# Feature-major rotation, score levels on more column groups and side-by-side gate products in a two-layer decoder trunk

## The chip, the core and the metric

The kernel runs on one core of one Trainium2 chip. The core has five instruction queues: TensorE (PE, matrix products into the PSUM banks), VectorE (DVE), ScalarE (ACT), GpSimd (POOL) and SyncE (SP, which here only starts DMAs). The metric is the device time of one execution in microseconds (us). All data are 32-bit floats, and the big products run as three products of split operands, as told below.

## The reference

A decoder trunk of two layers for one sequence of 1024 tokens and a model width of 1024. In each layer the normalised and modulated input is projected once, and four branches of four heads each read parts of that projection:

```
proj = jnp.einsum('bld,de->ble', h, w_in[layer])
y_a = hgrn2_branch(aq, af, ai, ag, ...)      # vector decay, exact within chunks
y_b = retention_branch(rq, rk, rv, rg, ...)  # scalar decay, rotary q and k
y_c = ssd_branch(...)                        # Mamba-2
y_d = gla_branch(gq, gk, gv, gg, glr, w_gk2, ...)
x = x + gate * jnp.einsum('ble,ed->bld', concat(y_a..y_d), w_out[layer])
```

Three of its formulas matter here. The rotation of the retention's q and k pairs feature d with feature d + 64 of a head of 128:

```
cat([t1 * cos - t2 * sin, t1 * sin + t2 * cos])
```

The gates of GLA come from a product of rank 16, `gk = lr_in @ w_gk2 + b_gk2` (16 columns into 256), and then `log_sigmoid(gk) / 16`. And the branches with a vector decay (HGRN2 and GLA) need scores in which each pair of positions s < t of a chunk has its own decay per channel; the kernel forms these by levels of blocks of size h = 1, 2, 4, ... 64: at each level the second half of every block of 2h looks at the first half.

## The kernel before

**Two kinds of projection.** A weight unit of 128 output columns can be projected feature-major (`proj_f`, L423): the result has features on the partitions and 512 tokens in each of two PSUM banks, by 48 matmuls of 512 columns (8 slices of the model width, 2 halves of the tokens, 3 products). Or 256 columns are projected token-major (`proj_t`, L454): tokens on the partitions, four PSUM banks, by 192 matmuls of 256 columns. The three products are hi times hi, hi times lo and lo times hi of the split weights (`split`, L402: ACT casts, DVE subtracts) and the split input (hh, hl). The PSUM pool `pp` has four banks for projections, for the output projection and a few transposes. Four more hold the mixers' products: tags `sc` (two), `po` and `ms` (one each). SBUF tiles of 128 x 1024 come from the pool `big` of eleven, tiles of 128 x 512 from `mid` of five.

**The order on TensorE is written by hand.** Projections and output projections are generators in a queue (`ready`); a mixer is a generator that yields a number of nanoseconds, and `fill` issues so much of the queue before the mixer goes on. So a mixer's small products stand between those of a projection, and a `yield 2500` means "issue about 2.5 us of queued products here". The other engines' queues are ordered by the scheduler of the framework.

**The retention branch, before.** `ret_qk` (L867) projects q and k of a head together, token-major, one `proj_t` of 256 columns. For each of four PSUM banks ACT copies q and k out (L877), DVE makes four products with cos and sin (L881 to L884, 128 x 128 each, twice), and POOL forms the difference and the sum (L885, L886). `ret_mix` (L891) then transposes q and k, 16 transposes of 128 x 128 on TensorE (L897) into `sc`, `ms`, `sc`, `po`, copies them out, scales k by its decay on DVE (L900), yields 1200, makes the scores (L910), multiplies them by the decay mask on DVE (L912) and goes into `scan` (L651), which makes the outputs and the running state. Each head's q and k are projected while the mixer of the head before runs: the queue holds `ret_qk` of the next head, then the projection of its v and gate (`vg_proj`). Head 0 is projected while the second group of the SSD branch runs in `ssd_mix` (L1028). There POOL weights the inputs of each chunk (L1069) and DVE carries the state (L1113 to L1127).

**Scores by levels, before.** `vector_scores` (L546) is called with one head of HGRN2 (nh = 1, moving operand 32 or 64 columns at the levels in question) and with two heads of GLA side by side (nh = 2, 64 or 128 columns). At h up to 16, keys of 32 positions are the weights, and the products of four blocks of a chunk go to PSUM partitions 0, 32, 64 and 96 (L584). At h = 32 (L592) they go to partitions 0 and 64 alone. At h = 64 (L601) all go to partitions 0 to 63, for GLA in two banks one after the other. ACT copies the results into the score matrix (L636, L641).

**Gates of GLA, before.** `gla_gates` (L756): 8 transposes (L762) bring the 16 columns onto partitions 0 to 15, ACT copies each half out, and after a `yield 900` four products of 16 rows by 512 columns follow (L777), each in its own bank of `sc`, with `yield 700` and two DVE instructions (L778, L779) behind each. Then ACT takes Exp and Ln, DVE subtracts (L786), ACT takes Exp again, and a `yield 8000` follows. The output projection, whose results DVE adds to the residual stream (L1164), is what fills these pauses.

**The end of a layer.** The last head of the retention, then the output projection of the last two branches' columns in `out_tiles` (L1171, products L1159), whose weights POOL multiplies by the gate (L1148).

Of the kernel before, what the change touches and what calls it, by code (L numbers as in the profile page):

```python
# [21 lines left out]
P = 128  # L22
# [6 lines left out]
C = 128  # L29
# [41 lines left out]
for _h in range(4):  # L71
    _t(("rqk", _h), RQ + 128 * _h, RK + 128 * _h)
    _t(("rvg", _h), RV + 128 * _h, RG + 128 * _h)
# [57 lines left out]
def shape_constants():  # L131
# [18 lines left out]
    ang = np.arange(L, dtype=np.float32)[:, None] * inv_freq[None, :]  # L150
    ang = ang.reshape(NT, P, 64).transpose(1, 0, 2).astype(np.float64)
    rot = np.stack([np.cos(ang), np.sin(ang)], axis=1).reshape(P, 2 * NT * 64)
    return out.astype(np.float32), rot.astype(np.float32), [float(np.exp(g * C)) for g in log_gamma]
# [13 lines left out]
def hybrid_trunk(ctx, nc, tc, t_in, out, gamma_c):  # L167
# [381 lines left out]
    def vector_scores(Q, Kt, f, nh, tiles, Dg, decay):  # L549
# [26 lines left out]
        for li, h in enumerate((1, 2, 4, 8, 16, 32, 64)):  # L576
            out_ = []
            if h <= 16:
                w = nh * 16
                ps = ps_mix("sc", 2)  # L580
                for c in range(NC):
                    for j in range(4):
                        s0 = c * C + 32 * j
                        pe.matmul(ps[32 * j : 32 * j + 32, c * w : c * w + w], Kt[:, s0 : s0 + 32],  # L584
                                  split2(q_at(s0, 32), h)[:, :, :, 1, :], start=True, stop=True)
            elif h == 32:
                w = nh * 32
                ps = ps_mix("sc", 2)
                for c in range(NC):
                    for b in range(2):  # L590
                        s0 = c * C + 64 * b
                        pe.matmul(ps[64 * b : 64 * b + 32, c * w : c * w + w], Kt[:, s0 : s0 + 32], q_at(s0 + 32, 32),  # L592
                                  start=True, stop=True)
            else:
                w = nh * 64
                for c0 in range(0, NC, NC // nh):
                    ps = ps_mix("sc", 2)
                    out_.append((c0, ps))
                    for i in range(NC // nh):
                        s0 = (c0 + i) * C  # L600
                        pe.matmul(ps[0:64, i * w : i * w + w], Kt[:, s0 : s0 + 64], q_at(s0 + 64, 64),  # L601
                                  start=True, stop=True)
            nb = L // (2 * h)
# [27 lines left out]
            elif h == 32:  # L631
                p4 = ps[:, 0 : NC * w].rearrange("p (c e t) -> p c e t", c=NC, e=nh)
                for e in range(nh):
                    for b in range(2):
                        pj = slice(64 * b, 64 * b + 32)
                        act.copy(tiles[e][pj, :, 64 * b + 32 : 64 * b + 64], p4[pj, :, e, :])  # L636
            else:
                for c0, ps in out_:
                    p4 = ps[0:64].rearrange("p (c e t) -> p c e t", c=NC // nh, e=nh)
                    for e in range(nh):  # L640
                        act.copy(tiles[e][0:64, c0 : c0 + NC // nh, 64:128], p4[:, :, e, :])  # L641
            yield 1700 + 300 * (nh - 1)
# [113 lines left out]
    def gla_gates(l, dl, wg, fs):  # L756

        lrT = []
        for half in range(2):
            ps = ps_mix("sc", 2)  # L760
            for i in range(4):
                pe.transpose(ps[0:16, i * P : (i + 1) * P], dl[:, half * 4 + i, 8:24], ident)  # L762
            lrT.append(mid_t()[0:16, :])
            act.copy(lrT[half], ps[0:16, :])
        yield 900
        mn = []
        nb = sm_t("nb", 2, bufs=1)
        vec.tensor_scalar(nb, col(("bgk", l)), -1.0, None, MUL)
        for p in range(2):
            f, m_ = big_t(), big_t()  # L770
# [3 lines left out]
            for half in range(2):  # L774
                s = slice(half * 512, half * 512 + 512)
                ps = ps_mix("sc", 2)
                pe.matmul(ps, wg[:, p * P : (p + 1) * P], lrT[half], start=True, stop=True)  # L777
                vec.tensor_scalar(m_[:, s], ps, b, 0.0, ADD, ALU.min)  # L778
# [81 lines left out]
    def ret_tables():  # L860
        rt = big_t()
        nc.sync.dma_start(rt, t_in["rot"])
        return (rt[:, 0:512].rearrange("p (m d) -> p m d", m=NT), rt[:, 512:1024].rearrange("p (m d) -> p m d", m=NT))

    def ret_qk(l, h, tables, u):
        if not tables:
            tables.extend(ret_tables())  # L867
        cos, sin = tables

        def ev(j, ps):  # L870
            if j == 0:
                u["q"], u["k"] = vg_tiles()
            ms_ = slice(2 * j, 2 * j + 2)
            c2 = cos[:, ms_, :]
            s2 = sin[:, ms_, :]
            for qk, o in (("q", 0), ("k", 128)):
                act.copy(u[qk][:, ms_, :], ps[:, :, o : o + 128])  # L877
            for qk in ("q", "k"):
                x1, x2 = u[qk][:, ms_, 0:64], u[qk][:, ms_, 64:128]
                t = mid_t().rearrange("p (i m d) -> p i m d", i=4, m=2)  # L880
                vec.tensor_tensor(t[:, 0], x1, c2, MUL)  # L881
                vec.tensor_tensor(t[:, 1], x2, s2, MUL)
                vec.tensor_tensor(t[:, 2], x1, s2, MUL)
                vec.tensor_tensor(t[:, 3], x2, c2, MUL)  # L884
                gp.tensor_tensor(u[qk][:, ms_, 0:64], t[:, 0], t[:, 1], SUB)  # L885
                gp.tensor_tensor(u[qk][:, ms_, 64:128], t[:, 2], t[:, 3], ADD)  # L886

        yield from proj_t(l, ("rqk", h), ev)

    def ret_mix(l, h, u, between=None):  # L890
        AT = ATs[h % 2]  # L891
        QT, KTt = big_t(), big_t()
        for half in range(2):
            for src, dst, tag in ((u["q"], QT, "sc"), (u["k"], KTt, ("ms", "po")[half])):
                ps = ps_mix(tag, 2 if tag == "sc" else 1)
                for i in range(4):
                    pe.transpose(ps[:, i * P : (i + 1) * P], src[:, half * 4 + i, :], ident)  # L897
                act.copy(dst[:, half * 512 : half * 512 + 512], ps)
        o, _ = CST["rke"]
        vec.tensor_scalar(u["k"], u["k"], cs[:, o + h : o + h + 1], None, MUL)  # L900
        ke = u["k"]
# [416 lines left out]
    for l in range(DEPTH):  # L1318
        more = l + 1 < DEPTH
        dl = dls[l]  # L1320
        wg = cst.tile([16, 256], F32, tag="wg", name=f"wg{l}")

# [4 lines left out]
        drain(p)  # L1327
        nc.sync.dma_start(wg, t_in["w_gk2"][l])
        steps = ssd_steps(l, dl, st)
# [172 lines left out]
```

## Time and profile before

Three runs before took 2083.15, 2083.54 and 2085.19 us, median 2083.54. The profiled execution is one of its own.

| what | value |
|---|---|
| profiled execution, its own time | 2084.53 us |
| its span, first to last instruction | 2082.7 us |
| so around the span | 1.8 us |
| median of three runs | 2083.54 us |
| profiled execution above the median | 1.0 us |
| granted TensorE clock, mean | 0.993 |
| HBM rate over the span | 58 GB/s |

How to read the rows: in the timeline a row is the start in us, the duration in us, engine, line, operation, out<-in, shapes and how many instructions were merged. A matmul's duration is a latency, since matmuls are pipelined: what one costs in a dense stream is the distance to the next one's start. A product of unsplit 32-bit floats shows as two instructions, a transpose as one. In the group rows stand the busy time, the mean ns of one instruction, and the idle time of the engine ahead of them with what ended it.

### The profile page before, as it was taken

To read this page: it belongs to the slowest core of one execution; us is meant where nothing else is said; L and a number is where in the kernel's file an instruction comes from. 1 tells how busy PE (TensorE), PEld (TensorE's weight loads), DVE (VectorE), ACT (ScalarE), POOL (GpSimd) and SP (SyncE) were. 2 spreads that over 40 slices of the span, in tenths; PEclk is the share of its full clock that TensorE was granted. 3 is DMA by queue.
4 is the path that set the end of the run, shared out by engine and by line. 5 is a ranking of instruction groups with operands and counts; after the bars stand their busy time and mean duration, and the time that the engine had idled before them with its cause. 6 is when DMAs were issued, how large, how long until landed. Compare 5 with 4: busy or idle time off the path is not lost.

```text
span 2082.7 us, 42807 instructions
## 1 busy us (share of the span) xinstructions
PE 2030.5 (97%) x17994; PEld 1822.1 (87%) x17994; DVE 1167.2 (56%) x2347; ACT 757.9 (36%) x1760; POOL 382.6 (18%) x564
## 2 busy tenths in 40 slices
PE   5999999999999999999999999999999999999997
PEld 4898888789888899999879888888988989999996
DVE  7656743836537476444555555356464565744456
ACT  7432223432345343122273223343234444322223
POOL 4101001000123233222220010010101323402232
PEclk9999999999999999999999999999999999999999
DMA  8233321111121120111112211111111212111112
GB/s 283 88 104 97 98 77 32 35 39 37 36 66 57 44 89 26 52 37 31 46 54 71 79 32 42 39 35 38 37 40 37 80 43 72 56 37 42 42 36 101
DMA packets 72304, 124.15 MB, mean 60 GB/s; under 512 B 10128, under 2 KB 20656, under 8 KB 72112
## 3 DMA queue, kind: packets, MB, share of 16 engines
q1 hardware_dynamic: 67216, 112.31, 17.6%
q10 hardware_dynamic: 4896, 9.12, 1.4%
q8 instruction: 141, 2.31, 0.5%
q14 instruction: 51, 0.42, 0.1%
HBM read 117.14 MB, written 4.26 MB: 58 GB/s over the span
## 4 chain that ended last, share of the span: by engine, by line
PE 85%; DVE 7%; ACT 4%; DMA 2%; issue 1%; POOL 1%; SPq 0%; POOLq 0%; ACTq 0%; DVEq 0%
PE pp L1159 14%; PE pp L467 12%; PE pp L469 11%; PE pp L470 11%; PE pp L420 7%; PE pp L422 6%; PE pp L421 6%; DMA wa<-in_w_ada 2%; PE sc L584 2%; PE sc L524 1%; DVE b L612 1%; PE po L1102 1%; PE ms L667 1%; PE pp L502 1%; DVE b L301 1%
## 5 line engine op out<-in xcount | busy, mean ns | idle before, releaser
L467 PE MATMUL pp<-whi,hh 128*128 128x256 f32 x2176 | 631.6, 290 | 0.7 <-ACT b L991 0.7
L469 PE MATMUL pp<-wlo,hh 128*128 128x256 f32 x2176 | 615.9, 283 | 0.0
L470 PE MATMUL pp<-whi,hl 128*128 128x256 f32 x2176 | 615.9, 283 | 0.0
L467 PEld LDWEIGHTS pp<-whi,hh 128*128 128x128 f32 x2176 | 417.2, 192 | 4.7 <-ACT b L991 1.5
L469 PEld LDWEIGHTS pp<-wlo,hh 128*128 128x128 f32 x2176 | 417.6, 192 | 0.5
L470 PEld LDWEIGHTS pp<-whi,hl 128*128 128x128 f32 x2176 | 417.1, 192 | 0.0
L405 ACT CAST whi<-raw 128x512 fp32r<-128x512 f32 x280 | 173.6, 623 | 593.9 <-PE pp L470 296.3
L406 DVE TENSOR_TENSOR wlo<-raw,whi 128x512 fp32r<-128x512 f32 x276 | 200.1, 729 | 282.2 <-ACT whi L405 275.2
L420 PE MATMUL pp<-hh,whi 128*128 128x512 f32 x640 | 268.2, 419 | 7.4 <-ACT hh L397 6.6
L422 PE MATMUL pp<-hl,whi 128*128 128x512 f32 x640 | 252.6, 395 | 1.4 <-DVE hl L398 1.3
L421 PE MATMUL pp<-hh,wlo 128*128 128x512 f32 x640 | 251.0, 392 | 0.0
L1164 DVE TENSOR_TENSOR xs<-xs,pp 128x512 f32<-128x512 f32 x256 | 172.9, 684 | 70.8 <-PE pp L1159 68.1
L1159 PE MATMUL pp<-whi,yh 128*128 128x512 f32 x448 | 188.4, 420 | 0.0
L1148 POOL TENSOR_TENSOR raw<-raw,gate_b 128x512 f32<-128x512 f32 x64 | 84.6, 1325 | 521.2 <-DMA raw<-in_w_out 407.3
L1159 PE MATMUL pp<-whi,yl 128*128 128x512 f32 x448 | 175.5, 392 | 0.0
L1159 PE MATMUL pp<-wlo,yh 128*128 128x512 f32 x448 | 174.9, 390 | 0.0
L420 PEld LDWEIGHTS pp<-hh,whi 128*128 128x128 f32 x640 | 120.9, 189 | 32.9 <-ACT hh L397 8.6
L422 PEld LDWEIGHTS pp<-hl,whi 128*128 128x128 f32 x640 | 120.6, 188 | 32.3 <-DVE hl L398 5.5
L421 PEld LDWEIGHTS pp<-hh,wlo 128*128 128x128 f32 x640 | 121.3, 190 | 20.1 <-DVE wlo L406 0.4
L272 POOL TENSOR_SCALAR rt<-ss 128x4 f32<-128x4 f32 (+1 forms) x46 | 12.2, 265 | 556.6 <-ACT junk L541 498.2
L301 DVE SCALAR_TENSOR_TENSOR b<-wa,c_act,b 128x512 f32<-128x512 f32 x84 | 71.2, 847 | 61.7 <-DMA wa<-in_w_ada 60.9
L1159 PEld LDWEIGHTS pp<-whi,yh 128*128 128x128 f32 x448 | 84.4, 188 | 21.1 <-issue 3.4
(257 smaller groups left out, 3075.4 us busy)
## 6 DMA issues: line engine op xcount, KB each, us to landing
raw<-in_wt SPq DMA_DIRECT2D x136, 256.0 KB, 3.0
wa<-in_w_ada SPq DMA_DIRECT2D x96, 256.0 KB, 2.9
raw<-in_wf SPq DMA_DIRECT2D x80, 256.0 KB, 2.6
raw<-in_w_out SPq DMA_DIRECT2D x64, 256.0 KB, 2.6
b<-cum ACTq DMA_DIRECT2D x32, 256.0 KB, 3.5
xs<-in_x SPq DMA_DIRECT2D x8, 512.0 KB, 8.1
out<-b SPq DMA_DIRECT2D x7, 512.0 KB, 2.6
b<-in_wt SPq DMA_DIRECT2D x4, 384.0 KB, 4.1
```

Of the source, the lines that this page charges most:

```text
L301: vec.scalar_tensor_tensor(acc, w, c_act[:, k : k + 1], acc, MUL, ADD)
L405: act.copy(hi, raw)
L406: eng.tensor_tensor(lo, raw, hi.bitcast(F32), SUB)
L420: pe.matmul(ps, hi[:, j : j + P], hh[half][:, k, :], start=(k == 0), stop=False)
L421: pe.matmul(ps, lo[:, j : j + P], hh[half][:, k, :], start=False, stop=False)
L422: pe.matmul(ps, hi[:, j : j + P], hl[half][:, k, :], start=False, stop=(k == KT - 1))
L467: pe.matmul(o, hhi, hi[:, j : j + 256], start=(k == 0 and m % 2 == 0), stop=False, skip_group_check=True)
L469: pe.matmul(o, hhi, lo[:, j : j + 256], start=False, stop=False, skip_group_check=True)
L470: pe.matmul(o, hlo, hi[:, j : j + 256], start=False, stop=(k == KT - 1), skip_group_check=True)
L1148: gp.tensor_tensor(raw, raw, gate_b[:, nh * 512 : (nh + 1) * 512], MUL)
L1159: pe.matmul(ps, a[:, o : o + P], b, start=(n == 0), stop=(n == 3 * len(kts) - 1))
L1164: vec.tensor_tensor(xv, xv, ps, ADD)
```

## The change

There are three edits, and each moves instructions.

**Rotation, feature-major.** q and k become feature-major units of their own (`rq`, `rk`, 48 matmuls of 512 columns each). The cos and sin tables are now two tiles, features by tokens, with the sign in the sine. For each bank ACT copies the two halves of 64 features crosswise into a `mid` tile, DVE multiplies the bank by cos, POOL multiplies the swapped tile by sin and adds it. `ret_mix` transposes k alone, and ACT applies the decay as it copies. Its `yield 1200` is gone.

**Score levels.** At h = 32 odd and even chunks go to partitions 0, 32, 64, 96 in turn; at h = 64 to 0 and 64 in turn, for GLA now in one bank. The copies out are split accordingly.

**Gates.** The 16 columns stand four times, at partitions 0, 32, 64 and 96, the weight likewise by halves (four small DMAs), and the four products stand side by side in four banks. The pauses are 2500, four times 700, 6000 between Ln and the subtraction, and 4000, instead of 900, four times 700 and 8000.

```diff
+    _f(("rq", _h), RQ + 128 * _h)
+    _f(("rk", _h), RK + 128 * _h)
...
         elif h == 32:
-                        pe.matmul(ps[64 * b : 64 * b + 32, c * w : c * w + w], Kt[:, s0 : s0 + 32], q_at(s0 + 32, 32),
+                        o, i = 64 * b + 32 * (c % 2), c // 2 * w
+                        pe.matmul(ps[o : o + 32, i : i + w], Kt[:, s0 : s0 + 32], q_at(s0 + 32, 32),
...
-                for c0 in range(0, NC, NC // nh):
-                    ps = ps_mix("sc", 2)
...
+                ps = ps_mix("sc", 2)
+                for c in range(NC):
+                    s0 = c * C
+                    o, i = 64 * (c % 2), c // 2 * w
+                    pe.matmul(ps[o : o + 64, i : i + w], Kt[:, s0 : s0 + 64], q_at(s0 + 64, 64), start=True, stop=True)
...
-        yield 900
+        yield 2500
...
+        pss = [ps_mix("po"), ps_mix("ms"), ps_mix("sc", 2), ps_mix("sc", 2)]
+        for i, ps in enumerate(pss):
+            o = 32 * i
+            pe.matmul(ps, wg[o : o + 16, :], lrT[o : o + 16, :], start=True, stop=True)
...
-                pe.matmul(ps, wg[:, p * P : (p + 1) * P], lrT[half], start=True, stop=True)
+                ps = pss[2 * p + half]
...
+        yield 6000
         for f, m_ in zip(fs, mn):
             vec.tensor_tensor(f, m_, f, SUB)
...
-        yield 8000
+        yield 4000
...
+        def ev(name):
+            def ev_(half, ps):
+                if half == 0:
+                    u[name] = big_t()
+                s = slice(half * 512, half * 512 + 512)
+                t = mid_t()
+                act.copy(t[0:64, :], ps[64:P, :])
+                act.copy(t[64:P, :], ps[0:64, :])
+                vec.tensor_tensor(u[name][:, s], ps, cos[:, s], MUL)
+                gp.tensor_tensor(t, t, sin[:, s], MUL)
+                gp.tensor_tensor(u[name][:, s], u[name][:, s], t, ADD)
+            return ev_
+        yield from proj_f(l, ("rq", h), ev("q"))
+        yield from proj_f(l, ("rk", h), ev("k"))
...
-        yield 1200
```

The first place is TensorE's queue at the start of the mixer of retention head 0 in layer 0. `sc`, `ms`, `po` are the mixers' banks, `pp` a bank of the output projection, `cs` holds the identity. Before, from the transposes to the first scores:

```order
L897 MATMUL sc_8986<-cs,b_1222_8607 128x128 x4
L897 MATMUL ms_8992<-cs,b_1223_8608 128x128 x4
L897 MATMUL sc_8998<-cs,b_1222_8607 128x128 x4
L897 MATMUL po_9004<-cs,b_1223_8608 128x128 x4
L1159 MATMUL pp_9025<-whi_9014,yh_8396 128x512
L1159 MATMUL pp_9025<-wlo_9015,yh_8396 128x512
L1159 MATMUL pp_9025<-whi_9014,yl_8397 128x512
L1159 MATMUL pp_9025<-whi_9021,yh_8442 128x512
L1159 MATMUL pp_9025<-wlo_9022,yh_8442 128x512
L1159 MATMUL pp_9025<-whi_9021,yl_8443 128x512
L910 MATMUL sc_9033<-b_1266_8984,b_1267_8985 128x128 x4
```

The same place in the changed kernel:

```order
L904 MATMUL ms_8873<-cs,b_1221_8551 128x128 x4
L904 MATMUL po_8879<-cs,b_1221_8551 128x128 x4
L914 MATMUL sc_8885<-b_1187_8389,b_1221_8551 128x128 x4
L1163 MATMUL pp_8905<-whi_8894,yh_8382 128x512
L1163 MATMUL pp_8905<-wlo_8895,yh_8382 128x512
L1163 MATMUL pp_8905<-whi_8894,yl_8383 128x512
```

Eight of the sixteen transposes are gone, and the first scores follow the rest directly.

The second place is TensorE's queue in the gates of layer 0, between products of the output projection. Before, the first two of the four products:

```order
L777 MATMUL sc_4235<-b_564_4200,wg_651 128x512
L1159 MATMUL pp_4239<-whi_4212,yh_3100 128x512
L1159 MATMUL pp_4239<-wlo_4213,yh_3100 128x512
L1159 MATMUL pp_4239<-whi_4212,yl_3101 128x512
L1159 MATMUL pp_4239<-whi_4219,yh_4030 128x512
L1159 MATMUL pp_4239<-wlo_4220,yh_4030 128x512
L1159 MATMUL pp_4239<-whi_4219,yl_4031 128x512
L777 MATMUL sc_4247<-b_566_4207,wg_651 128x512
```

Now all four:

```order
L1163 MATMUL pp_4247<-whi_4235,yl_4046 128x512
L774 MATMUL po_4257<-b_563_4210,wg_651 128x512
L774 MATMUL ms_4258<-b_563_4210,wg_651 128x512
L774 MATMUL sc_4259<-b_563_4210,wg_651 128x512
L774 MATMUL sc_4260<-b_563_4210,wg_651 128x512
L1163 MATMUL pp_4269<-whi_4228,yh_3112 128x512
```

The four products, which read four partition ranges of one tile, now follow each other; before, six products of the output projection stood between any two.

The third place is POOL's queue while the second SSD group of layer 0 runs and q and k of retention head 0 are projected. `s` are the weighted inputs of the SSD chunks (of one chunk by dt, dw and rbdsk), `b` the retention's tiles. Before, from the last chunk on:

```order
L1069 TENSOR_TENSOR s_1220_8592<-b_1077_7701,dt_1171 128x128
L1069 TENSOR_TENSOR s_1220_8592<-b_1098_7944,dt_1171 128x128
L1069 TENSOR_TENSOR s_1221_8593<-b_1077_7701,rbdsk_1144 128x128
L1069 TENSOR_TENSOR s_1221_8593<-b_1098_7944,rbdsk_1144 128x128
L1148 TENSOR_TENSOR raw_9011<-raw_9011,gate_b 128x512
L885 TENSOR_TENSOR b_1222_8607<-b_1224_8611 128x2x64
L886 TENSOR_TENSOR b_1222_8607<-b_1224_8611 128x2x64
```

Now, from the first rotation (of q) to the next chunk's inputs:

```order
L888 TENSOR_TENSOR b_1188_8390<-b_1188_8390,b_1173_8310 128x512
L889 TENSOR_TENSOR b_1187_8389<-b_1187_8389,b_1188_8390 128x512
L888 TENSOR_TENSOR b_1189_8399<-b_1189_8399,b_1173_8310 128x512
L889 TENSOR_TENSOR b_1187_8389<-b_1187_8389,b_1189_8399 128x512
L1073 TENSOR_TENSOR s_1202_8446<-b_1074_7723,rbdsk_1150 128x128
L1073 TENSOR_TENSOR s_1202_8446<-b_1095_7966,rbdsk_1150 128x128
L1073 TENSOR_TENSOR s_1213_8505<-b_1074_7723,dt_1177 128x128
```

All of the rotation stood behind the last chunk's inputs; now q's four instructions stand ahead of the inputs of later chunks, and k's four stand where the sixteen stood.

More of the change, by code (lines that the diff above doesn't have):

```diff
@@ L576, in vector_scores @@
         for li, h in enumerate((1, 2, 4, 8, 16, 32, 64)):
-            out_ = []
             if h <= 16:
@@ L595, in vector_scores @@
                 w = nh * 64
-                for c0 in range(0, NC, NC // nh):
-                    ps = ps_mix("sc", 2)
[L598 to L602, printed above, removed]
+                ps = ps_mix("sc", 2)
[3 more added lines that the diff above has]
+                    pe.matmul(ps[o : o + 64, i : i + w], Kt[:, s0 : s0 + 64], q_at(s0 + 64, 64), start=True, stop=True)
             nb = L // (2 * h)
@@ L756, in gla_gates @@
     def gla_gates(l, dl, wg, fs):
-        lrT = []
+        lrT = mid_t()
         for half in range(2):
@@ L762, in gla_gates @@
                 pe.transpose(ps[0:16, i * P : (i + 1) * P], dl[:, half * 4 + i, 8:24], ident)
-            lrT.append(mid_t()[0:16, :])
-            act.copy(lrT[half], ps[0:16, :])
-        yield 900
-        mn = []
+            for p in range(2):
+                o = 64 * p + 32 * half
+                act.copy(lrT[o : o + 16, :], ps[0:16, :])
+        yield 2500
         nb = sm_t("nb", 2, bufs=1)
         vec.tensor_scalar(nb, col(("bgk", l)), -1.0, None, MUL)
+        pss = [ps_mix("po"), ps_mix("ms"), ps_mix("sc", 2), ps_mix("sc", 2)]
+        for i, ps in enumerate(pss):
+            o = 32 * i
+            pe.matmul(ps, wg[o : o + 16, :], lrT[o : o + 16, :], start=True, stop=True)
+        mn = []
         for p in range(2):
@@ L860, in ret_tables @@
     def ret_tables():
-        rt = big_t()
-        nc.sync.dma_start(rt, t_in["rot"])
-        return (rt[:, 0:512].rearrange("p (m d) -> p m d", m=NT), rt[:, 512:1024].rearrange("p (m d) -> p m d", m=NT))
+        rt = [big_t(), big_t()]
+        for i in range(2):
+            nc.sync.dma_start(rt[i], t_in["rot"][i])
+        return rt
     def ret_qk(l, h, tables, u):
@@ L868, in ret_qk @@
         cos, sin = tables
[L870 to L886, printed above, removed]
@@ L890, in ret_mix @@
+        yield from proj_f(l, ("rq", h), ev("q"))
+        yield from proj_f(l, ("rk", h), ev("k"))
     def ret_mix(l, h, u, between=None):
         AT = ATs[h % 2]
-        QT, KTt = big_t(), big_t()
+        QT, KTt = u["q"], u["k"]
+        o, _ = CST["rke"]
+        ke = big_t().rearrange("p (c d) -> p c d", c=NC)
         for half in range(2):
[L894 to L898, printed above, removed]
@@ L899, in ret_mix @@
-        o, _ = CST["rke"]
-        vec.tensor_scalar(u["k"], u["k"], cs[:, o + h : o + h + 1], None, MUL)
-        ke = u["k"]
+            ps = ps_mix(("ms", "po")[half])
+            for i in range(4):
+                c = half * 4 + i
+                pe.transpose(ps[:, i * P : (i + 1) * P], KTt[:, c * C : (c + 1) * C], ident)
+            act.activation(ke[:, half * 4 : half * 4 + 4, :], ps.rearrange("p (c d) -> p c d", c=4), AF.Copy,
+                           scale=cs[:, o + h : o + h + 1])
@@ L1327, in hybrid_trunk @@
         drain(p)
-        nc.sync.dma_start(wg, t_in["w_gk2"][l])
+        for i in range(4):
+            nc.sync.dma_start(wg[32 * i : 32 * i + 16, :], t_in["w_gk2"][l, :, (i // 2) * P : (i // 2 + 1) * P])
         steps = ssd_steps(l, dl, st)
```

26 lines of the change are left out of this document (13 added, 13 removed).

## The prediction

> **What bounds the kernel now.** I read the busy times of the engines first, then the chain that ended last, then TensorE's own waits. The page's parts 1 and 4:
>
> ```profile
> PE 2030.5 (97%) x17994; PEld 1822.1 (87%) x17994; DVE 1167.2 (56%) x2347; ACT 757.9 (36%) x1760; POOL 382.6 (18%) x564
> ...
> PE 85%; DVE 7%; ACT 4%; DMA 2%; issue 1%; POOL 1%; SPq 0%; POOLq 0%; ACTq 0%; DVEq 0%
> ```
>
> TensorE's waits, the first row, with total, number and longest:
>
> ```profile
> PE pp L380 <- DMA xs<-in_x: 13.7, 1, 13.7
> ```
>
> TensorE is busy or in the chain nearly all the time, and its largest wait is the one for the first input. So the kernel is as long as the list of TensorE's instructions, and each edit is priced by the distance between starts on TensorE. The other engines count only where they make it wait.
>
> **The projections of q and k.** Dense stretches of both forms, first and last row of each, in the timeline of TensorE:
>
> ```profile
> 879.93 0.28 PE L469 MATMUL pp<-wlo,hh 128*128 128x256 f32 x1
> ...
> 890.85 0.28 PE L470 MATMUL pp<-whi,hl 128*128 128x256 f32 x1
> ```
>
> ```profile
> 566.47 0.39 PE L421 MATMUL pp<-hh,wlo 128*128 128x512 f32 x1
> ...
> 579.64 0.39 PE L422 MATMUL pp<-hl,whi 128*128 128x512 f32 x1
> ```
>
> The first stretch has 91 steps in 10.92 us, 0.120 each; the second 58 in 13.17 us, 0.227 each. A head's q and k cost 192 x 0.120 = 23.0 us before and 2 x 48 x 0.227 = 21.8 us after: 1.24 us less, 9.9 us for eight heads. The Trainium skill ("TensorE: Matmul & The Clock Gate", section "Back-to-back issue gap") gives N/2.4 + 2.5 ns for a warm matmul of N columns, so 109 and 216 ns. By it a head would save 192 x 109 - 96 x 216 = 0.2 us, 1.5 us in all. The trace's steps are both about 11 ns longer, and a fixed cost per instruction counts twice as often in the token-major form; I take the trace.
>
> **The transposes.** The block in front of the scores, and the next stream's first row:
>
> ```profile
> 890.97 0.60 PE L897 MATMUL sc<-cs,b 128*128 128x128 f32 x4
> ...
> 892.63 0.36 PE L467 MATMUL pp<-whi,hh 128*128 128x256 f32 x1
> ```
>
> Sixteen transposes take 1.66 us; eight go, 0.83 us per head, 6.6 us in all. The copies behind them shrink likewise, off the path.
>
> **The score levels.** One HGRN2 call, then one GLA call, each level's block with the start of what follows it:
>
> ```profile
> 171.58 0.70 PE L592 MATMUL sc<-b,b 128*32 128x32 f32 x32
> 172.21 0.50 PE L420 MATMUL pp<-hh,whi 128*128 128x512 f32 x1
> ...
> 174.48 1.15 PE L601 MATMUL sc<-b,b 128*64 128x64 f32 x16
> 175.55 0.50 PE L420 MATMUL pp<-hh,whi 128*128 128x512 f32 x1
> ```
>
> ```profile
> 408.66 1.09 PE L592 MATMUL sc<-b,b 128*32 128x64 f32 x32
> 409.68 0.39 PE L467 MATMUL pp<-whi,hh 128*128 128x256 f32 x1
> ...
> 412.39 1.09 PE L601 MATMUL sc<-b,b 128*64 128x128 f32 x8
> 413.69 1.09 PE L601 MATMUL sc<-b,b 128*64 128x128 f32 x8 [0.22 <-ACT at L636]
> 414.71 0.39 PE L467 MATMUL pp<-whi,hh 128*128 128x256 f32 x1
> ```
>
> Two blocks of before show what more column groups are worth. L836 has the instructions of GLA's L601 (16 of 64 weight columns by 128) but alternates between partitions 0 and 64; L566 has the instructions of GLA's L592, twice as many, on four groups:
>
> ```profile
> 429.37 1.09 PE L836 MATMUL ms<-b,b 128*64 128x128 f32 x16
> 430.40 0.50 PE L420 MATMUL pp<-hh,whi 128*128 128x512 f32 x1
> ```
>
> ```profile
> 385.20 1.10 PE L566 MATMUL sc<-b,b 128*32 128x64 f32 x64
> 386.23 0.50 PE L1159 MATMUL pp<-whi,yh 128*128 128x512 f32 x1
> ```
>
> L836 takes 1.03 us where GLA's L601 takes 2.32, and L566 brings 64 instructions through in 1.03 where L592 needs 1.02 for 32. So GLA's h = 64 falls by 1.29, four calls, 5.2 us, the wait for ACT between its two banks among it. Its h = 32 halves, less a fixed start: 0.45 x 4 = 1.8. HGRN2 has eight calls: of 1.07 about half, 0.50 x 8 = 4.0, and of 0.63 about 0.25 x 8 = 2.0. Together 13.0 us. ACT has more and shorter copies, with a pause of 1700 or more behind each level to hide them; without it a call waited some tenths, as the 0.22 above.
>
> **The gates.** One of the four products, with the stream's rows around it, then three products of GLA's scan that use 64 rows each, even ones on partitions 0 to 63, odd ones on the others:
>
> ```profile
> 365.51 0.40 PE L1159 MATMUL pp<-whi,yl 128*128 128x512 f32 x1
> 365.84 1.12 PE L777 MATMUL sc<-b,wg 16*128 16x512 f32 x2
> 366.89 0.50 PE L1159 MATMUL pp<-whi,yh 128*128 128x512 f32 x1
> 367.23 0.40 PE L1159 MATMUL pp<-wlo,yh 128*128 128x512 f32 x1
> ```
>
> ```profile
> 434.96 0.27 PE L849 MATMUL po<-st,b 64*128 64x128 f32 x1
> 434.96 0.27 PE L849 MATMUL sc<-st,b 64*128 64x128 f32 x1
> 435.07 0.27 PE L849 MATMUL po<-st,b 64*128 64x128 f32 x1
> ```
>
> A product takes 1.05 us, and breaking the stream costs 0.33 - 0.23 = 0.10 before it and 0.34 - 0.23 = 0.11 behind it: 1.26. Products on different rows and banks start together, those on the same rows 0.11 us apart, so I take four at the price of one: 3 x 1.26 = 3.8 us per layer, 7.6 in all. No row shows four ranges at once; at worst only the breaks go, 3 x 0.21 x 2 = 1.3.
>
> **Waits that go.** At the layer's end, and in an SSD chunk:
>
> ```profile
> 1033.70 0.61 PE L1159 MATMUL pp<-whi,y 128*128 128x512 f32 x2
> 1036.18 0.50 PE L1159 MATMUL pp<-wlo,y 128*128 128x512 f32 x1 [1.87 <-DVE wlo L406]
> ```
>
> ```profile
> 789.45 0.74 PE L1102 MATMUL po<-s,b 128*128 128x64 f32 x5 [0.77 <-DVE s L1120]
> ```
>
> In the first, weights are split behind the last head's norm on DVE. Without the pause of 1200 one more unit of the queue, 6 x 0.227 = 1.4 us, lies between that norm and the need; but DVE then has one more addition ahead of the split, about half of it. I take 0.7 per layer, 1.4; the bounds are 0 and 3.7. In the second, DVE frees a bank late because the rotation's small instructions stand before it; they are gone: 0.77 per layer, 1.5.
>
> **Waits that come.** The groups that POOL and ACT pay or stop paying (count, busy, mean ns):
>
> ```profile
> L1148 POOL TENSOR_TENSOR raw<-raw,gate_b 128x512 f32<-128x512 f32 x64 | 84.6, 1325 | 521.2 <-DMA raw<-in_w_out 407.3 <-ACT b L650 59.2 <-DVE b L737 17.8
> L885 POOL TENSOR_TENSOR b<-b 128x128 f32<-128x128 f32 x64 | 44.1, 689 | 90.0 <-DVE b L883 89.2 <-ACT b L877 0.6 <-ACT whi L405 0.3
> L886 POOL TENSOR_TENSOR b<-b 128x128 f32<-128x128 f32 x64 | 34.5, 540 | 0.0
> ...
> L798 ACT COPY b<-pp 64x512 f32<-64x512 f32 x8 | 4.6, 580 | 15.5 <-PE pp L422 15.4
> ```
>
> POOL's new instructions have L1148's form: 64 x 1.33 = 85 us instead of 44 + 35 = 79, nothing in sum. But q's four, 5.3 us, now stand among the inputs of the SSD chunks, and k's before the last part. What waits is the state on DVE, then the chunk's products on TensorE. The nearest row is the 0.77 just shown; I take it for q and k, in two layers: 3.1 us, between 0 and twice that. In the gates all eight DVE instructions now come in one piece, and the second subtraction waits for ACT's two Ln with the residual additions queued behind it; TensorE meets them after four banks. The added pause of 6000 is meant for just that place, but the scheduler still puts that subtraction four additions after the last gate instruction. Between 0 and 1.87, the longest wait above, I take 0.9 per layer: 1.8. The copies of GLA's columns double to four; the pause that grew from 900 to 2500 hides them, and without it two more copies of 0.58 would cost 1.2 us per layer. A second table of 512 KB goes through SP behind q's two weight loads. The page's part 6 has a load of that size, with the us to its landing:
>
> ```profile
> xs<-in_x SPq DMA_DIRECT2D x8, 512.0 KB, 8.1
> ```
>
> Half of q's and k's projection, 10.9 us, lies between those loads and the first use of the table or of a later weight, so it costs nothing; without that cover it would be the 8.1 once per layer.
>
> **The sum.** 9.9 + 6.6 + 13.0 + 7.6 + 1.4 + 1.5 = 40.0 us gained, 3.1 + 1.8 = 4.9 lost, net 35.1. The profiled execution took 2084.53, so 2049.4 for one like it; it lay 1.0 above the median, so 2048.4.
>
> **The rivals.** *Groups do not overlap.* Odd and even chunks have the weights of one product each, and a product shows two instructions on the same group in a row, so pairs might not meet. Then the levels keep 13.0 but for the wait between GLA's banks (1.30 - 1.03 = 0.27 a call, 1.1), the gates save 1.3 instead of 7.6: 18.2 us lost, 2066.6. Against it L836, whose products alternate the same way. Chance 0.06.
>
> *A bank comes free late.* The projection of v and gate starts with four banks, the third 12 x 0.120 = 1.4 us after k's last product; ACT owes k's two banks four copies of 0.58, which end at about 1.9 if ACT is free, for a fourth bank needed at 2.2. If a weight's split or a norm stands between, TensorE waits about 1.2 us per head: 9.6, 2058.0. Chance 0.13.
>
> *Only columns cost.* If a stream ran at the skill's rate above (the same title and section), 8.4 us of the first term would be lost. As a mechanism of this kernel: equal columns, equal time, 2056.8. The two stretches speak against it. Chance 0.02.
>
> *POOL is late, and the kernel slower.* Three rows of POOL and DVE at the rotation of before:
>
> ```profile
> 790.79 2.80 POOL L885 TENSOR_TENSOR b<-b 128x128 f32<-128x128 f32 x1 [1.67 <-DVE b L883]
> ```
>
> ```profile
> 784.21 0.28 DVE L881 TENSOR_TENSOR b<-b,b 128x128 f32<-128x128 f32 x1
> 784.41 0.54 DVE L882 TENSOR_TENSOR b<-b,b 128x128 f32<-128x128 f32 x1
> ```
>
> One operation took 2.80 us, four times its mean, and equal DVE instructions took 0.28 or 0.54. If all eight of a head took 4 x 1.33, they would need 43 us, against 10.9 + 23.0 = 34 us from q's end to the mixer: 9 us late per head, 2048.4 + 72 = 2120. It decides slower than before from 34 / 8 + 39 / 64 = 4.9 us each. Against it: 128 operations have means of 0.69 and 0.54, and the many DVE instructions beside that one go. The Trainium skill ("GPSIMD Engine Reference", section "Key points") says that POOL shares its SBUF interfaces with DVE, with contention when DVE has two SBUF inputs, and that DVE is about twice as fast for elementwise work; the 0.54 and 1325 ns agree, and it speaks against adding here. But the new DVE product reads PSUM. Chance 0.02.
>
> **Numbers.** The forecast has 0.75, the rest 0.02 is what I have not thought of. Range: below, no new waits and the layer-end wait wholly gone, 2048.4 - 4.9 - 2.3 = 2041; above, late banks and a few more of the waits above, 2062. About 0.2% is what a measurement here can tell from no change, 4 us. Faster 0.96, same 0.01, slower 0.03.
>
> **What would show it.** L592 and L601 blocks of about half the length; one block of gates of 1.1 to 1.3 us per layer; dense steps still 0.120 and 0.227; eight transposes of 0.83 us before the scores. Wrong would be a large wait of TensorE on ACT or DVE at the start of v's projection, on POOL ahead of `po` in the second SSD group, or on scores of a head whose q and k are late.

## The result and the profile after

The changed kernel takes 2047.61 us (median, 2046.24 to 2049.05) against 2083.35 of the kernel before: ratio 0.9828, 95% interval 0.9811 to 0.9845. Forecast were 2048.4 us, 35.1 less than before; measured are 35.7, and in the profiled execution 36.4 (span 2046.3 against 2082.7).

The page of the changed kernel, parts 1 and 4:

```profile
PE 1997.6 (98%) x17162; PEld 1762.0 (86%) x17162; DVE 1115.8 (55%) x2115; ACT 779.7 (38%) x1788; POOL 394.9 (19%) x500
...
PE 88%; ACT 5%; DVE 4%; DMA 2%; issue 1%; POOL 0%; POOLq 0%; SPq 0%; ACTq 0%; DVEq 0%
```

TensorE has lost 832 instructions and 33 us of busy time and is 98% busy instead of 97: still the list of TensorE's instructions sets the time.

The blocks that the prediction priced, in TensorE's timeline (L594 is the level h = 32, L602 h = 64, L774 the gates' products, L904 the transposes of retention, L1163 the output projection):

```profile
171.19 0.46 PE L594 MATMUL sc<-b,b 128*32 128x32 f32 x32
171.58 0.50 PE L422 MATMUL pp<-hh,whi 128*128 128x512 f32 x1
...
173.84 0.69 PE L602 MATMUL sc<-b,b 128*64 128x64 f32 x16
174.46 0.50 PE L422 MATMUL pp<-hh,whi 128*128 128x512 f32 x1
...
362.92 0.69 PE L774 MATMUL po<-b,wg 16*128 16x512 f32 x1
...
362.93 0.70 PE L774 MATMUL sc<-b,wg 16*128 16x512 f32 x2
...
363.99 0.50 PE L1163 MATMUL pp<-whi,yh 128*128 128x512 f32 x1
...
377.29 0.50 PE L1163 MATMUL pp<-whi,yh 128*128 128x512 f32 x1 [0.77 <-DVE xs L1168]
...
379.64 0.50 PE L1163 MATMUL pp<-whi,yh 128*128 128x512 f32 x1 [0.67 <-DVE xs L1168]
...
405.75 0.65 PE L594 MATMUL sc<-b,b 128*32 128x64 f32 x32
406.34 0.39 PE L469 MATMUL pp<-whi,hh 128*128 128x256 f32 x1
...
409.05 1.09 PE L602 MATMUL sc<-b,b 128*64 128x128 f32 x16
410.07 0.39 PE L469 MATMUL pp<-whi,hh 128*128 128x256 f32 x1
...
855.51 0.28 PE L472 MATMUL pp<-whi,hl 128*128 128x256 f32 x1
856.01 0.39 PE L469 MATMUL pp<-whi,hh 128*128 128x256 f32 x1 [0.22 <-DVE b L887]
...
876.98 0.60 PE L904 MATMUL ms<-cs,b 128*128 128x128 f32 x4
...
877.85 1.06 PE L914 MATMUL sc<-b,b 128*128 128x128 f32 x8
...
984.56 0.60 PE L904 MATMUL ms<-cs,b 128*128 128x128 f32 x4
...
1017.47 0.50 PE L1163 MATMUL pp<-wlo,y 128*128 128x512 f32 x1 [1.11 <-DVE wlo L408]
```

From the start of a block to the start of what follows, HGRN2's levels take 0.39 and 0.62 us (0.63 and 1.07 before), GLA's first call 0.59 and 1.02 (1.02 and 2.32). In GLA's second call of the layer, where ScalarE's copy held the second bank up longer before, the level h = 64 went from 2.86 to 1.25. Over all twelve calls the blocks are 13.1 us shorter. All four gate products are through in 1.07, where one took 1.05. Eight transposes take 0.87. From layer 0's second retention head to its fourth (984.56 - 876.98) it is 53.8 us a head. The same two places of before, the first of which the prediction shows as 890.97, give 55.3:

```profile
1001.60 0.60 PE L897 MATMUL sc<-cs,b 128*128 128x128 f32 x4
```

By stages, the gain of the profiled execution and what the forecast had for each (its terms summed for the place; the stages are cut at starts of the same instructions in both traces):

| stage | forecast per layer | layer 0 | layer 1 |
|---|---|---|---|
| HGRN2, to the end of its part | 3.0 | 2.8 | 2.7 |
| gates and GLA | 6.4 | 6.7 | 4.0 |
| SSD and retention | 7.4 | 8.4 | 7.4 |
| layer's end | 0.7 | 2.4 | 2.0 |

Of the 2.0 in layer 1, 0.8 is the wait for a weight. The other 1.2 lies behind the last matmul, which started 10.0 us before the end of the span and now starts 8.8 before it: VectorE makes the last residual addition 0.4 us after that start, where it was 2.7 late before. No edit was meant for that.

### The profile page after: what moved, and what is told of

The parts are those of the page before. It is cut to its first block, busy times and chain, and to the rows that moved or that the text cites. A ratio compares the mean times of both kernels' runs of the same rounds, so it can differ in the third digit from the quotient of the medians.

```text
span 2046.3 us, 40860 instructions
## 1 busy us (share of the span) xinstructions
PE 1997.6 (98%) x17162; PEld 1762.0 (86%) x17162; DVE 1115.8 (55%) x2115; ACT 779.7 (38%) x1788; POOL 394.9 (19%) x500
## 4 chain that ended last, share of the span: by engine, by line
PE 88%; ACT 5%; DVE 4%; DMA 2%; issue 1%; POOL 0%; POOLq 0%; SPq 0%; ACTq 0%; DVEq 0%
PE pp L1163 15%; PE pp L422 10%; PE pp L469 10%; PE pp L424 9%; PE pp L423 9%; PE pp L472 9%; PE pp L471 9%; PE sc L585 2%; PE sc L526 1%; PE po L1106 1%; DMA wa<-in_w_ada 1%; PE ms L669 1%; PE pp L504 1%; PE pp L505 1%; PE pp L506 1%
## 5 line engine op out<-in xcount | busy, mean ns | idle before, releaser
L469 PE MATMUL pp<-whi,hh 128*128 128x256 f32 x1664 | 481.6, 289 | 1.2 <-ACT b L995 0.7
L471 PE MATMUL pp<-wlo,hh 128*128 128x256 f32 x1664 | 471.2, 283 | 0.0
L472 PE MATMUL pp<-whi,hl 128*128 128x256 f32 x1664 | 471.2, 283 | 0.0
L422 PE MATMUL pp<-hh,whi 128*128 128x512 f32 x896 | 374.7, 418 | 7.5 <-ACT hh L399 6.7
L424 PE MATMUL pp<-hl,whi 128*128 128x512 f32 x896 | 353.0, 394 | 1.4 <-DVE hl L400 1.4
L423 PE MATMUL pp<-hh,wlo 128*128 128x512 f32 x896 | 350.8, 392 | 0.0
L469 PEld LDWEIGHTS pp<-whi,hh 128*128 128x128 f32 x1664 | 319.3, 192 | 6.6 <-DVE b L887 1.6
L471 PEld LDWEIGHTS pp<-wlo,hh 128*128 128x128 f32 x1664 | 319.6, 192 | 0.7
L472 PEld LDWEIGHTS pp<-whi,hl 128*128 128x128 f32 x1664 | 319.3, 192 | 0.0
L423 PEld LDWEIGHTS pp<-hh,wlo 128*128 128x128 f32 x896 | 169.6, 189 | 28.0 <-DVE wlo L408 0.4
L1163 PE MATMUL pp<-whi,yh 128*128 128x512 f32 x448 | 187.6, 419 | 2.9 <-DVE xs L1168 2.9
L1163 PE MATMUL pp<-whi,yl 128*128 128x512 f32 x448 | 175.5, 392 | 0.0
L1163 PE MATMUL pp<-wlo,yh 128*128 128x512 f32 x448 | 174.8, 390 | 0.0
L1163 PEld LDWEIGHTS pp<-whi,yh 128*128 128x128 f32 x448 | 84.4, 188 | 21.5 <-DVE xs L1168 4.6
```

The lines of the kernel that those rows point to most:

```text
L422: pe.matmul(ps, hi[:, j : j + P], hh[half][:, k, :], start=(k == 0), stop=False)
L423: pe.matmul(ps, lo[:, j : j + P], hh[half][:, k, :], start=False, stop=False)
L424: pe.matmul(ps, hi[:, j : j + P], hl[half][:, k, :], start=False, stop=(k == KT - 1))
L469: pe.matmul(o, hhi, hi[:, j : j + 256], start=(k == 0 and m % 2 == 0), stop=False, skip_group_check=True)
L471: pe.matmul(o, hhi, lo[:, j : j + 256], start=False, stop=False, skip_group_check=True)
L472: pe.matmul(o, hlo, hi[:, j : j + 256], start=False, stop=(k == KT - 1), skip_group_check=True)
```

## The experiments

Each version has four or five times (`gates_alone` eleven), and their median is given; the kernel before took 2083.60 to 2084.16 beside them. The number in brackets behind a ratio is its 95% interval.

**One part alone, in the kernel before.** The edits are the three parts of the diff shown above, each by itself.

> Only the feature-major rotation is put into the kernel before. My theory: its share is the 9.9 us of the projections, 6.6 of the transposes, 1.5 of the SSD wait and 1.4 at the layer's end, and nothing of the 3.1 that I forecast for GpSimd among the SSD chunks, since the changed kernel's trace has no such wait: 19.4 us less, 2064. Rival one, the wait on GpSimd is there but something else of the change covers it: 16.3 less, 2067. Rival two, equal columns cost equal time: 11 less, 2072.

Measured: 2064.62 us, ratio 0.9904 (0.9889 to 0.992), 19.0 less. The first theory holds; 16.3 is just outside the interval (16.7 to 23.1 less), 11 far outside.

> Only the wide score levels are put into the kernel before. My theory: neighbours on different column groups run at once, 13.0 us less, 2070.4. Rival: the shorter blocks only bring the next wait on ScalarE forward, and the levels keep less than half, 2077 or more.

Measured: 2074.68 us, ratio 0.9957 (0.9944 to 0.9969), 8.9 less, between 6.5 and 11.7. The blocks shrank as in the whole change, but what came behind them took a part back. Of the waits of TensorE in this kernel (total, times, longest) one row was not there before; the changed kernel has it too:

```profile
PE sc L649 <- ACT at L641: 1.8, 4, 0.6
```

The transposes of GLA's keys follow the level h = 64 through the same two `sc` banks. The block now ends 1.3 us sooner, ACT's copies out of the bank do not, and the transposes meet a bank that is still being read. So the rival had the mechanism, and the theory most of the size: the blocks give 13.1, and those transposes lose some 2 of it. The rest of the difference to 8.9 lies within the interval.

> Only the gates' products side by side, with the moved pauses, are put into the kernel before. My theory from the changed kernel's trace: 7.6 us of products and breaks gained, two waits for VectorE of together 1.76 us per layer lost, 4.1 us less, 2079.3. Rival: the waits for VectorE come from the whole change (shorter levels, more ScalarE copies around them), then this part alone keeps the 5.8 that I forecast or up to 7.6, 2075.8 to 2077.6. If the three parts are independent, their gains sum to the 35.7 of the whole.

Measured: 2080.32 us, ratio 0.9981 (0.9973 to 0.999), 3.3 less. Its waits are those of the whole change, to the tenth; the first row is of this kernel's waits, the others of the changed one's:

```profile
PE pp L1164 <- DVE xs L1169: 2.9, 4, 0.8
```

```profile
PE pp L1163 <- DVE xs L1168: 2.9, 4, 0.8
...
PE sc L651 <- ACT at L643: 1.2, 2, 0.6
```

So they belong to the gates, not to what stands around them. The three parts alone sum to 31.2; the whole gives 35.7 with an interval of 32 to 39. Within the three intervals that is a sum, and no larger interaction is needed or excluded.

**Which neighbours run at once.** The order of the chunks is changed in `vector_scores`. `group_order` changes it at both wide levels, and at h = 32 it also takes the first blocks of all chunks ahead of the second ones (first cut below); `pair_order` changes h = 64 alone:

```diff
-                for c in range(NC):
-                    for b in range(2):
+                for b in range(2):
+                    for c in (0, 2, 4, 6, 1, 3, 5, 7):
...
-                for c in range(NC):
+                for c in (0, 2, 4, 6, 1, 3, 5, 7):
```

> The changed kernel, its two wide levels issued in another order: first all products of one column group, then all of the next, same instructions and same banks. My theory: two products run at once only when they stand next to each other in TensorE's order on different groups; then the blocks go back to nearly the length of before, 0.45 x 8 and 0.25 x 8 for HGRN2, 1.03 x 4 and 0.45 x 4 for GLA: 11.5 us more than the changed kernel, 2059. Rival: each group has a queue of its own and the order does not matter, 2047.6.

```diff
-                for c in range(NC):
+                for c in (0, 2, 1, 3, 4, 6, 5, 7):
                     s0 = c * C
                     o, i = 64 * (c % 2), c // 2 * w
```

> The changed kernel, level h = 64 alone in another order: chunks 0, 2, 1, 3, 4, 6, 5, 7, so two products of one column group in a row. My theory from group_order's starts, where the second group began when three instructions of the first were still to start: TensorE looks some three instructions ahead, so runs of four instructions still overlap nearly whole; GLA's block 1.2 us at most instead of 1.02, the kernel within 1.5 of the changed one, 2047.6 to 2049. Rival: only direct neighbours run at once; GLA's block is then about 1.6 and HGRN2's 0.9, 0.6 x 4 + 0.3 x 8 = 4.8 more, 2052.4.

Measured: 2056.08 and 2047.62 us, ratios 0.9866 (0.9853 to 0.988) and 0.9829 (0.9816 to 0.9843). GLA's block at h = 64, grouped and in pairs:

```profile
412.96 1.58 PE L602 MATMUL sc<-b,b 128*64 128x128 f32 x16
414.47 0.39 PE L469 MATMUL pp<-whi,hh 128*128 128x256 f32 x1
```

```profile
407.41 1.15 PE L602 MATMUL sc<-b,b 128*64 128x128 f32 x16
408.49 0.39 PE L469 MATMUL pp<-whi,hh 128*128 128x256 f32 x1
```

Alternating, with two instructions of one group in a row, the block takes 1.02 us, in runs of four instructions 1.08, in runs of eight 1.51. Without any overlap it would be at most twice the 1.02 that eight in a row took before. Neither theory of `group_order` was right: order matters, but TensorE begins an instruction on the free group while a few of the other group's (three, by the starts in the trace of `group_order`) still wait ahead of it. So runs of eight lose about half of the overlap and runs of four nearly nothing. At h = 32 I had overlooked that my order also put four products, eight instructions, of one group together where the kernel before alternated, so that level became longer than before (0.83 us against 0.63 in HGRN2). Over all calls the blocks of `group_order` are 10.5 us longer than the changed kernel's, and the 1.6 us that the transposes of GLA's keys lose there is gone, so 8.9; measured are 8.5 more.

**The gates' rows.** All four products read the same 16 partitions:

```diff
-            pe.matmul(ps, wg[o : o + 16, :], lrT[o : o + 16, :], start=True, stop=True)
+            pe.matmul(ps, wg[0:16, (i // 2) * P : (i // 2 + 1) * P], (lrT, lr2)[i % 2][0:16, :], start=True, stop=True)
```

> The changed kernel, with all four gate products on the same 16 partitions, still issued one behind another into four banks. My theory: the products ran at once only because they read four ranges of rows; now they take 1.05 us each, three more per layer, 6.3 us more than the changed kernel, 2053.9. Rival: what the change saved was only the breaks in the stream, which are still saved here; then it stays within 1.3, 2047.6 to 2049.

Measured: 2050.82 us, ratio 0.9839 (0.9826 to 0.9852), 3.2 more than the changed kernel. The products in this kernel's timeline:

```profile
363.37 1.12 PE L772 MATMUL po<-b,wg 16*128 16x512 f32 x2
364.34 1.02 PE L772 MATMUL ms<-b,wg 16*128 16x512 f32 x2
365.19 1.88 PE L772 MATMUL sc<-b,wg 16*128 16x512 f32 x4
367.00 0.50 PE L1161 MATMUL pp<-whi,yh 128*128 128x512 f32 x1
```

The block is 3.63 us instead of 1.07, 5.1 for two layers, a little under my 6.3. The separate row ranges are what made them run at once, as forecast. But TensorE has no wait for the residual additions here at all: what the products lose comes back in part, since VectorE has caught up by then. Layer 0 shows this alone; in layer 1 TensorE also ran at a lower clock behind the products (last section), which gave VectorE more time. Put the other way, some 3.5 of the 7.6 that the gates save on TensorE were only time for VectorE.

**GpSimd's load doubled.**

```diff
-                gp.tensor_tensor(t, t, sin[:, s], MUL)
+                for _ in range(3):
+                    gp.tensor_tensor(t, t, sin[:, s], MUL)
```

> The changed kernel, its product with sin on GpSimd done three times in place instead of once, so that GpSimd has 16 instead of 8 operations of 1.3 us per retention head; the rotation is no longer the reference's. My theory: GpSimd's part has slack, the head's projection of v and gate lies behind it; at most the wait among the SSD chunks that I forecast for the single work now shows, 3.1: 2047.6 to 2050.7. Rival, GpSimd is close to late: each head then waits some of the added 10.6 us, half of it would be 42, 2090.

Measured: 2068.99 us, ratio 0.9929 (0.9916 to 0.9943), 21.4 more than the changed kernel. My theory fell: there is far less slack than I said. Three rows of this kernel's waits of TensorE:

```profile
PE po L1107 <- DVE s L1125: 8.0, 2, 4.0
...
PE sc L526 <- DVE b L547: 4.9, 4, 1.3
...
PE pp L469 <- DVE b L887: 2.8, 4, 1.2
```

The first is the wait that the prediction put at 0.77, in the SSD chunks, and it now has 4.0 us a layer. GpSimd's timeline at that place, doubled and then as changed, from the first operation of q's rotation to the first input of the chunk:

```profile
758.02 6.84 POOL L889 TENSOR_TENSOR b<-b,b 128x512 f32<-128x512 f32 x5 [7.43 <-ACT b L886]
...
769.15 0.76 POOL L1074 TENSOR_TENSOR s<-b,rbdsk 128x128 f32<-128x128 f32 x2
```

```profile
759.82 1.29 POOL L888 TENSOR_TENSOR b<-b,b 128x512 f32<-128x512 f32 x1 [7.42 <-ACT b L886]
...
765.48 0.76 POOL L1073 TENSOR_TENSOR s<-b,rbdsk 128x128 f32<-128x128 f32 x2
```

From the one to the other it is 11.1 us instead of 5.7, 5.5 more, of which TensorE waits for 4.0. So q's rotation in front of the inputs fits as it is, with some 1.5 us to spare, about one operation. The other two rows are the heads. GpSimd makes two small operations of each head's norm, and they now stand behind a longer rotation of q:

```profile
911.87 0.27 POOL L274 TENSOR_SCALAR rt<-ss,cs 128x4 f32<-128x4 f32 x1
```

VectorE waits 8.91 us for them, so the transposes of the head's output come late (second row). Behind that norm on VectorE stand the products with cos that free k's banks, so the projection of v finds its bank late (third row), the place of the rival "a bank comes free late". The two additional waits of 4.0 cost more than themselves: TensorE's granted clock is 0.65 and 0.67 in the two stretches of 5 us from 775 us on, and 0.69 and 0.63 from 1785 on, which is 3.4 us each time. The three rows, 15.3 us more than in the changed kernel, and this clock together make up the 21.4.

**Where the gates' wait comes from.** The timelines of VectorE and of ScalarE in the changed kernel there:

```profile
371.20 1.22 DVE L793 TENSOR_TENSOR b<-b,b 128x1024 f32<-128x1024 f32 x1
372.34 1.28 DVE L1168 TENSOR_TENSOR xs<-xs,pp 128x512 f32<-128x512 f32 x2
375.42 1.23 DVE L793 TENSOR_TENSOR b<-b,b 128x1024 f32<-128x1024 f32 x1 [1.80 <-ACT b L790]
376.56 0.68 DVE L1168 TENSOR_TENSOR xs<-xs,pp 128x512 f32<-128x512 f32 x1
378.30 0.69 DVE L408 TENSOR_TENSOR wlo<-raw,whi 128x512 fp32r<-128x512 f32 x1 [1.06 <-ACT whi L407]
```

```profile
370.56 1.28 ACT L788 ACT_TABLE_LOAD   x1
...
373.03 1.28 ACT L790 ACT_TABLE_LOAD   x1
```

The second subtraction waits 1.80 us for the second Ln, and the first late residual addition stands right behind it. The second late one stands behind the low part of a weight, whose cast came late on ScalarE (1.06), behind the first of the last two Exp. Exp and Ln take turns there, so each pays its table load of 1.28. The Trainium skill ("ScalarE: Activation LUTs", section "Table sets: the hidden batching unit") has a set that holds both functions, with which no load would be needed between them; these rows have one at every turn, so that set is not the one in use here. Three orders were tried. First ScalarE alone as written:

```diff
+        with tc.manual_schedule(engines={nc.scalar.engine}):
             for p, f in enumerate(fs):
                 act.activation(f, f, AF.Exp, bias=nb[:, p : p + 1])
             for f in fs:
                 act.activation(f, f, AF.Ln, bias=1.0)
```

> The changed kernel with ScalarE kept to the written order in the gates: Exp, Exp, Ln, Ln, so three table loads per layer instead of five; VectorE's order stays as good as it was. My theory: the 1.76 us per layer come from VectorE standing at the second subtraction, which waits for the second Ln; the fewer loads bring that only some 0.3 forward, since the second Exp waits for VectorE anyway, so less than half of the wait goes: 2046 to 2047.6. Rival: the table loads on ScalarE are the cause, and the wait goes with them: 2044.

Then the whole part from the products to the last Exp as written, on both engines, and on VectorE alone:

```diff
+        with tc.manual_schedule(engines={nc.vector.engine, nc.scalar.engine}):
```

> The changed kernel with VectorE and ScalarE kept to the written order in the gates, so that the pause of 6000 really puts the residual additions ahead of the two subtractions. My theory: the waits of TensorE for the additions go, 2 x 1.76 = 3.5 us less, 2044.1. Rival: the eight instructions of the gates on VectorE are themselves what holds the additions up, wherever the subtractions stand; then nothing changes, 2047.6.

```diff
+        with tc.manual_schedule(engines={nc.vector.engine}):
```

> The changed kernel with VectorE alone kept to the written order in the gates; ScalarE keeps its own order, with the weights' casts ahead of the last Exp. My theory after written_order: the waits for the residual additions go there too, and the 4.5 us per layer that took their place came from the casts behind the two Ln; with the casts left free both are gone, 3.5 us less than the changed kernel, 2044.1. Rival: on VectorE the split of a weight behind the additions comes late as well, and TensorE waits there: 2050 or more.

Measured: 2045.09, 2056.53 and 2047.45 us, ratios 0.9814 (0.98 to 0.9827), 0.9869 (0.9856 to 0.9883) and 0.9827 (0.9814 to 0.9841). TensorE's one long wait of the place in each, in the same order:

```profile
374.61 0.50 PE L1164 MATMUL pp<-whi,yh 128*128 128x512 f32 x1 [1.01 <-DVE xs L1169]
```

```profile
377.03 0.79 PE L1164 MATMUL pp<-whi,yh 128*128 128x512 f32 x1 [4.33 <-ACT whi L407]
```

```profile
372.40 0.50 PE L1164 MATMUL pp<-wlo,yh 128*128 128x512 f32 x1 [1.50 <-DVE wlo L408]
```

With fewer table loads one wait of about 1 us is left of two. With the subtractions really behind the additions, no addition is late, but the next weight is: its cast stands behind both Ln on ScalarE (4.33), or its low part behind the additions on VectorE (1.50). So each theory was half of it. The gates' work on the two engines delays whatever stands behind it, and moving one instruction back brings another to the front. Only `written_order` differs from the changed kernel by more than the intervals: 8.9 us slower, by its two waits of 4.33 and by half clock behind each (0.50 from 377 to 382 us). The 2.5 us of `scalar_order` lie within them. Which order would leave no wait was not found.

**Two more waits mended.**

```diff
+        yield 1500
         ke = u["ke"] = big_t()
...
-            w.append(split(raw, 512))
+            w.append(split(raw, 512, gp if kts == (6, 7) and nh and kt == 6 else vec))
```

> vector_written_order, and two more places mended: a pause of 1500 ahead of the transposes of GLA's keys (0.8 us of wait in the second call of each layer), and at the layer's end the low part of one weight of the last projection made on GpSimd, which is idle there (1.27 of wait per layer). My theory: 3.5 + 1.6 + about 1.5 of the 2.5 less, 2041. Rival: the waits only move to the next place, 2044 or more.

> scalar_order, with the same two mends. My theory: 1.2 + 1.6 + 1.5 less than the changed kernel, 2043.3; if the time of scalar_order stands as measured, 2042. Rival: the waits only move, 2045 or more.

Measured: 2043.97 and 2042.94 us, ratios 0.9809 (0.9796 to 0.9823) and 0.9806 (0.9792 to 0.9819). The first is 3 us over its forecast, because its part on VectorE's order gave nothing (2047.45 alone); the second is as forecast. What each of the two mends gives alone was not run. In the second's waits of TensorE, GLA's keys no longer wait for ScalarE, and these two rows are left of what was 2.9 and, at the layer's end, 2.2:

```profile
PE pp L1165 <- DVE xs L1170: 2.0, 2, 1.0
...
PE pp L1165 <- DVE wlo L408: 0.5, 2, 0.3
```

With 2042.77 to 2044.42 it lies below every run of the changed kernel, 4.7 us by the medians, and is the fastest version here.

## Why the prediction was right

- **What bounds it.** Right: the busy time of TensorE fell by 33 of the 36 us.
- **Projections and transposes, 16.5.** The steps were right, the sum too large. From mixer to mixer 1.5 us came off instead of 1.24 + 0.83. By the stages, SSD and retention brought 15.8 in both layers together; without the 2.8 that the SSD's waits gave (below) that is 13.0 for this term. Eight transposes are 0.87, as priced. What is missing is in the projections: the 512-column stream that the head's mixer breaks up runs at some 0.231 where I took the 0.227 of an undisturbed stretch, 0.4 us for the 96 products of a head, and once in each layer v's projection waits for a bank (0.50 from 855.51 to 856.01 instead of 0.12).
- **Score levels, 13.0.** The two calls that the prediction shows give 8 x (0.24 + 0.45) + 4 x (0.43 + 1.30) = 12.4, and all twelve 13.1, since GLA's second call gained more. Right in mechanism and size. Not seen was the wait behind them, at GLA's keys in the second call of each layer, 1.6 in all. I had named ACT's pause of 1700 as the cover; it covers the copies within the levels, but the transposes behind the last level come too soon.
- **Gates, 7.6 gained.** Right: four products at the price of one, though no row before showed four ranges at once. `one_row_range` shows that the ranges do it.
- **Gates' wait, 1.8 lost.** The mechanism was right for the first of two waits; the second, behind a late weight, was not named. The size was not right: TensorE's steps show 0.93 and 0.83 a layer, 3.5 in all. I had bounded it by 1.87 a layer and taken half.
- **Layer's end, 1.4 gained.** Right: 1.87 became 1.11, so 1.5 for two layers.
- **SSD wait, 1.5 gained, and GpSimd, 3.1 lost.** The first went: by TensorE's steps it was 0.93 a layer, 1.9 in all. With it, in layer 0, went a wait that the prediction did not name, at the transposes of the SSD's output (four of them took 1.29 us from 800.92 in the kernel before, with TensorE idle for 0.55 until VectorE's norm was done, and take 0.36 now), another 0.9. The loss to GpSimd did not come. `gpsimd_doubled` shows that GpSimd's load in the SSD was the right place and has a real price, 4.0 a layer when doubled, but that the single work still fits.
- **Rivals.** Groups that do not overlap: refuted by the blocks. A late bank: it came, but with 0.4 us in one head of each layer instead of 1.2 in every head. Columns alone: in the changed kernel, too, 256 columns take 0.12 and 512 take 0.23. A late GpSimd: not at the present load.

Three errors, 3.5 too much for retention, 1.7 too little for the gates' wait and 1.6 for the wait at GLA's keys, were made up by the 3.1 that did not come, by 1.3 more from the SSD's waits, by the clock (1.7, below) and by the 1.2 behind the last matmul; less than 1 us of the profiled gain is left that no row assigns. That these cancel, and so the closeness of 2047.6 to 2048.4, is partly luck.

## What to carry to other kernels

Where one engine's list of instructions sets the time, price an edit by the distance between starts on that engine, and then look at the next user of each buffer that it frees sooner: here GLA's shorter levels ran into ScalarE's copies, the shorter gates into VectorE's additions, and v's projection into k's banks. Small products overlap if they stand on different column groups or row ranges within a few instructions of each other, so alternate them or use pairs. A cover must be tested by more load and not by the absence of a wait: GpSimd caused none, and had about one operation to spare.

## What the runs showed of the hardware

TensorE's granted clock falls to a half for some 3.4 us behind some waits of less than 2 us. In the kernel before, after the wait of 1.87 at layer 0's end, it is 0.50 from 1037.6 to 1040.9 us (the third number from the end of the row; ahead of it the busy time of each engine). In its timeline there, steps of 512 columns are 0.43 us instead of 0.23:

```profile
1037.60:1040.90 3.30, 3.30 (x10) 2.53 (x9) 1.38 (x2) 1.15 (x2) 0.00 (x0) 0.50 0.38 133
```

```profile
1038.21 1.05 PE L1159 MATMUL pp<-whi,y 128*128 128x512 f32 x2
1039.06 0.63 PE L1159 MATMUL pp<-wlo,y 128*128 128x512 f32 x1
```

Over the ten microseconds from 1035 the clock is 0.76 and 0.90, so that costs 0.24 x 5 + 0.10 x 5 = 1.7 us. In the changed kernel it happened in layer 1, behind a wait of 1.76 for the SSD's running sums, and not behind the same wait in layer 0:

```profile
1350.08 0.27 PE L969 MATMUL ms<-cs,b 64*128 64x64 f32 x1 [1.76 <-DVE b L968]
...
1351.81 0.41 PE L469 MATMUL pp<-whi,hh 128*128 128x256 f32 x1
```

Behind the first 100 us and ahead of the end, the profiled executions have none (`scalar_order`, `all_mended`) to three such places. That is why the layer's end gained 2.4 us in layer 0 of the table and not 0.7, and why gates and GLA gained 6.7 in one layer and 4.0 in the other: the kernel before had its slow stretch in layer 0 there, the changed one in layer 1. The Trainium skill ("TensorE: Matmul & The Clock Gate", section "What's actually happening") has a gate that judges activity in free-running windows of about 3.4 us and gives half clock after an idle one. The two levels and the length agree; but here a wait of 1.8 us inside busy work was enough, in some places and not in others. Nor does it take a wait: in layer 1 of `one_row_range` the four gate products of 16 rows follow the stream without a gap, from 1362.77 us on, and behind them TensorE is busy all the time at a clock of 0.53, for 6.8 us in all:

```profile
1365.00:1370.00 5.00, 5.00 (x10) 2.65 (x9) 3.23 (x5) 3.12 (x3) 0.00 (x0) 0.53 0.16 45
```

The same products in layer 0 had no such stretch behind them. Whether removing the SSD's wait would also remove the slow stretches was not tried; `scalar_order` and `all_mended` still have that wait and show none.
